# PSUM banks shared anew in a two-layer diffusion step: two banks for the prompt and the score tiles, two for the latents' single-bank products

## The chip, the cores and the metric

The kernel runs on one core of one Trainium2 chip. The metric is the device time of one execution in microseconds (us). Engines are named as in the profile: PE (TensorE matmul), PEld (its weight loads), DVE (VectorE), ACT (ScalarE), POOL (GpSimd) and SP (SyncE, which here only issues DMAs).

## The reference, cut to what matters

Two token streams go through the same two layers: 128 prompt tokens and 512 latent tokens, 1024 wide. Each layer has four mixers side by side (latent attention, a Fourier transform, gated linear attention, windowed attention), a gated merge, and a PEER block that scores every token against 16384 experts and mixes the top 16 of each of 8 heads.

```python
u = layer_norm(x) * (1 + sc1) + sh1
parts = split(u @ w_in)                  # q, k, v, gates of the four mixers
o_a, o_b, o_c, o_d = mla(parts), fourier(parts), gla(parts), swa(parts)
mix = sum(sigmoid(gate_n) * (o_n @ w_branch[n]) for n in range(4)) @ w_out
x = layer_norm(alpha * x + g1 * mix)
u = layer_norm(x) * (1 + sc2) + sh2
sc = einsum(u @ w_peer_q, peer_keys)     # two score tables of 128 keys per head
idx, w = top16(v1 + v2)
x = layer_norm(alpha * x + g2 * (w * gelu(u @ peer_u[idx])) @ peer_v[idx])
```

## The kernel before, in words

The latents come first in the program, and the prompt is a generator that is stepped beside them: each large product of the latents calls `hook()`, which adds to a credit, and for each whole credit one piece of the prompt's work is written into the program. A scheduler then orders every instruction of an engine by priority. The prompt's dense pieces of layer 0 have a priority raised by 1000, its gathers one lowered by 300; in layer 1 both are lowered. An engine runs its instructions strictly in the order that results, so an instruction that waits holds everything behind it on that engine.

PSUM has eight banks of 128x512 f32. Four of them are two double-bank buffers (`P2`: attention scores, transposes, the dense expert weights, most of the PEER output). The other four are shared between two pools. `P1` gives single-bank buffers to the latents: the 24-matmul products against streamed weights (`gemm_T`, L361), the gate product and the branch product of each merge step (L698 and L703), the root-mean-square sums (L616), the decay inputs of the gated linear attention (L793), the output projection (L1021), the scores of the PEER keys (L1115), the modulation vectors ("ada", L437), and two of the six PEER output tiles (`pout`, L1360). `PP` gives single-bank buffers to the prompt. A buffer is given out again when its last reader, on ACT or DVE, is done.

The stages of a layer for the latents: modulation and layer norm (`ln_mod`), the mixers, `attn_out`, again `ln_mod`, the choice of experts (`peer_top`: 16 products, each followed by four small score matmuls and by a selection on DVE), `wdense` (a dense matrix of expert weights, through DRAM), and the stream over 128 blocks of experts (`s_stage`, `v_stage`, `v_mm`), in which `psS` holds the scores of one block and is kept for the whole stream. In the stream the latents use `psS` and the six output tiles and nothing else.

The lines that hand out the buffers, and the one that chooses where `psS` lies:

```python
    psg = pool("psg", 4 - NPP, space=PSUM)
    psp = pool("psp", NPP, space=PSUM)
        sps = PP("psS") if NPP > 1 else P1("psS")
```

Of the kernel before, what the change touches and what calls it, by code (L numbers as in the profile page):

```python
# [49 lines left out]
SCB = 6  # L50
LND = 2
NLN = (0, 0)
NPP = 1
WPAD = 128
FILL = (2, 6)
AQ = (1, 0)
# [187 lines left out]
def build(tc, A, O, layers=L, tap=None, stop=None):  # L244
# [4 lines left out]
    def pool(name, bufs, st=top, **k):  # L249
        return st.enter_context(tc.tile_pool(name=name, bufs=bufs, **k))  # L250
# [25 lines left out]
    pss = pool("pss", 2, space=PSUM)  # L276
    psg = pool("psg", 4 - NPP, space=PSUM)
    psp = pool("psp", NPP, space=PSUM)

# [3 lines left out]
    def P1(name="p1"):  # L283
        return psg.tile([128, 512], F32, name=name, tag="g")

    def PP(name="pp"):
        return psp.tile([128, 512], F32, name=name, tag="p")
# [1001 lines left out]
    def early(l, i):  # L1289
        return NGEL - 2 + i * ((128 - NGEL + 2) // max(NEA[l], 1))  # L1290
# [34 lines left out]
    def peer(l, u, pre, raw, acc):  # L1325
# [11 lines left out]
        at = {early(l, i): i for i in range(NEA[l])}  # L1337
        sps = PP("psS") if NPP > 1 else P1("psS")
        with tc.tile_pool(name=f"wb{l}", bufs=1) as wb:
# [659 lines left out]
```

## Time and profile before

| | us |
|---|---|
| three runs, median (lowest to highest) | 4385.21 (4367.93 to 4387.62) |
| the profiled execution: its own time | 4379.12 |
| its span | 4377.0 |
| PE busy | 4177.1 |
| DVE busy | 3496.4 |
| ACT busy | 1805.2 |
| POOL busy | 1386.3 |

The profile is one execution. Its span is what the trace covers; 2.1 us lie around it. The trace shows an f32 matmul as two records, so a group of 8 records of L1556 is four matmuls. A row of the timeline ends, in brackets, with the engine's idle time before it and what ended it.

### The profile page before, as it was taken

To read this page: it belongs to the slowest core of one execution; us is meant where nothing else is said; L and a number is where in the kernel's file an instruction comes from. 1 tells how busy PE (TensorE), PEld (TensorE's weight loads), DVE (VectorE), ACT (ScalarE), POOL (GpSimd) and SP (SyncE) were. 2 spreads that over 40 slices of the span, in tenths; PEclk is the share of its full clock that TensorE was granted. 3 is DMA by queue.
4 is the path that set the end of the run, shared out by engine and by line. 5 is a ranking of instruction groups with operands and counts; after the bars stand their busy time and mean duration, and the time that the engine had idled before them with its cause. 6 is when DMAs were issued, how large, how long until landed. Compare 5 with 4: busy or idle time off the path is not lost.

```text
span 4377.0 us, 60083 instructions
## 1 busy us (share of the span) xinstructions
PE 4177.1 (95%) x21118; PEld 3324.1 (76%) x21118; DVE 3496.4 (80%) x7100; ACT 1805.2 (41%) x3109; POOL 1386.3 (32%) x1033
## 2 busy tenths in 40 slices
PE   8999999899799999999999999998889999999998
PEld 4557777674599999888886667776568889889897
DVE  3347878799898888777777687788999988878887
ACT  3344343447543333433335443434485433333333
POOL 0000433100254445244440044230004654445541
PEclk9999999999899999999999999999989999999999
DMA  7663756546899999899996576474269999999996
GB/s 247 214 211 117 260 194 212 191 131 241 302 366 338 345 343 342 278 359 337 353 351 212 174 253 224 165 233 160 82 246 345 372 369 319 335 331 348 359 333 210
DMA packets 440126, 1182.17 MB, mean 270 GB/s; under 512 B 42656, under 2 KB 152944, under 8 KB 436496
## 3 DMA queue, kind: packets, MB, share of 16 engines
q1 hardware_dynamic: 279168, 625.44, 41.1%
q0 software_dynamic: 147744, 538.10, 34.7%
q10 hardware_dynamic: 12912, 14.79, 1.0%
q8 instruction: 166, 2.72, 0.2%
q14 instruction: 136, 1.11, 0.1%
HBM read 1115.98 MB, written 62.19 MB: 269 GB/s over the span
## 4 chain that ended last, share of the span: by engine, by line
PE 67%; DVE 10%; DMA 5%; issue 3%; ACT 3%; POOL 1%; ACTq 0%; SPq 0%; DVEq 0%; POOLq 0%
PE psS L1303 23%; PE pout L1322 23%; PE p L361 8%; PE psada L444 2%; PE psw L1202 2%; DMA wraw<-in_peer_v_dram 2%; PE p L708 1%; DVE wlo L256 1%; DVE eq L256 1%; PE pp L1476 1%; PE pp L1556 1%; DMA row<-in_peer_u_dram,pidx 1%; PE p L538 1%; PE pss L673 1%; DVE y L265 1%
## 5 line engine op out<-in xcount | busy, mean ns | idle before, releaser
L350 ACT CAST whi<-wraw 128x1024 fp32r<-128x1024 f32 x694 | 728.1, 1050 | 1055.9 <-PE psS L1303 615.6
L256 DVE TENSOR_TENSOR wlo<-wraw,whi 128x1024 fp32r<-128x1024 f32 x694 | 846.6, 1220 | 385.1 <-ACT whi L350 334.4
L1303 PE MATMUL psS<-u,whi 128*128 128x384 f32 x4032 | 1051.3, 341 | 23.5 <-ACT gel L253 21.5
L1303 PEld LDWEIGHTS psS<-u,whi 128*128 128x128 f32 x4032 | 739.7, 190 | 52.2 <-ACT gel L253 27.7
L1303 PE MATMUL psS<-u,wlo 128*128 128x384 f32 x2016 | 686.3, 340 | 2.3 <-DVE wlo L256 2.3
L1218 POOL DMA_INDIRECT row<-in_peer_u_dram,pidx x256 | 325.7, 1272 | 1124.5 <-ACT pidx L1097 651.2
L361 PE MATMUL p<-u,whi 128*128 128x512 f32 (+1 forms) x1760 | 593.9, 412 | 0.7 <-DVE rt L256 0.4
L1218 POOL DMA_INDIRECT row<-in_peer_u_dram,idg x256 | 370.6, 1448 | 597.1 <-DVE dots L1229 361.0
L1218 POOL DMA_INDIRECT row<-in_peer_v_dram,pidx x256 | 323.7, 1264 | 679.0 <-DVE pacc L1235 180.0
L1218 POOL DMA_INDIRECT row<-in_peer_v_dram,idg x256 | 363.1, 1419 | 521.5 <-DVE accs L1235 443.2
L1322 PE MATMUL pout<-whi,ph 128*128 128x512 f32 x1536 | 507.5, 407 | 1.0 <-ACT whi L350 1.0
L1322 PE MATMUL pout<-wlo,ph 128*128 128x512 f32 x1536 | 501.5, 404 | 0.1
L1322 PE MATMUL pout<-whi,pl 128*128 128x512 f32 x1536 | 490.0, 398 | 0.0
L361 PEld LDWEIGHTS p<-u,whi 128*128 128x128 f32 (+1 forms) x1760 | 327.4, 190 | 88.4 <-issue 15.7
L1303 PEld LDWEIGHTS psS<-u,wlo 128*128 128x128 f32 x2016 | 381.9, 189 | 3.4 <-DVE wlo L256 2.9
L1314 ACT CAST ph<-gel 128x384 fp32r<-128x384 f32 x256 | 131.5, 514 | 574.1 <-PE pout L1322 551.9
L361 PE MATMUL p<-u,wlo 128*128 128x512 f32 (+1 forms) x880 | 360.3, 409 | 7.9 <-DVE wlo L256 7.9
L1235 DVE SCALAR_TENSOR_TENSOR pacc<-row,pdots,pacc 128x1024 f32<-128x1024 f32 x254 | 324.9, 1279 | 37.5 <-PE p L361 27.2
L1229 DVE CUSTOM_DVE_ANT_0 row<-row,pu 128x1024 f32<-128x1024 f32 x256 | 309.9, 1218 | 48.9 <-DMA row<-in_peer_u_dram,pidx 27.4
L1322 PEld LDWEIGHTS pout<-wlo,ph 128*128 128x128 f32 x1536 | 288.0, 188 | 77.2 <-issue 12.3
L1322 PEld LDWEIGHTS pout<-whi,pl 128*128 128x128 f32 x1536 | 287.7, 188 | 71.5 <-issue 4.4
L1322 PEld LDWEIGHTS pout<-whi,ph 128*128 128x128 f32 x1536 | 285.8, 188 | 59.5 <-issue 10.9
(511 smaller groups left out, 6377.2 us busy)
## 6 DMA issues: line engine op xcount, KB each, us to landing
wraw<-in_peer_ut_dram SPq DMA_DIRECT2D x256, 512.0 KB
wraw<-in_peer_v_dram SPq DMA_DIRECT2D x256, 512.0 KB
wraw<-in_w_ada_dram SPq DMA_DIRECT2D x96, 512.0 KB
wraw<-in_w_in_dram SPq DMA_DIRECT2D x96, 512.0 KB
big<-wst SPq DMA_DIRECT2D x64, 768.0 KB
pw<-in_w_gt_dram SPq DMA_DIRECT2D x128, 256.0 KB
wst<-stg SPq DMA_DIRECT2D x12, 2048.0 KB
wst<-big SPq DMA_DIRECT2D x12, 2048.0 KB
```

The costliest lines, as they stand in the source:

```text
L256: V.tensor_tensor(out=out, in0=a, in1=b, op=op)
L265: V.scalar_tensor_tensor(out=out, in0=a, scalar=s, in1=b, op0=op0, op1=op1, **k)
L350: S.copy(hi, raw)
L361: i = PE.matmul(ps[:m, :T], a[:, o:o + m], b[:, k], start=(n == 0), stop=(n == 3 * KD - 1))
L444: PE.matmul(ps[:r, :256], (s4 if split else cth)[:, 4 * hf + k, :], w[:, k * 256:(k + 1) * 256], start=(n == 0), stop=(not isg and hf == 1 ...
L1202: PE.matmul(ps[:, t * 128:(t + 1) * 128], at(oa, t), at(w, t), start=(n == 0), stop=(n == 1))
L1218: pace(G.indirect_dma_start(out=t, out_offset=None, in_=A[src], in_offset=bass.IndirectOffsetOnAxis(ap=ix, axis=0)), lags[0])
L1229: return V.tensor_tensor_reduce(out=t, in0=t, in1=x, scale=1.0, scalar=0.0, op0=ALU.mult, op1=ALU.add, accum_out=dst)
L1235: return V.scalar_tensor_tensor(out=acc, in0=t, scalar=ge, in1=acc, op0=ALU.mult, op1=ALU.add)
L1303: PE.matmul(ps, a[:, k * 128:(k + 1) * 128], b[:, k, 128:T], start=(n == 0), stop=(n == 3 * KD - 1))
L1314: S.copy(ph, ge)
L1322: PE.matmul(outs[d][hf], a[:, d * 128:(d + 1) * 128], b[:, hf * 512:(hf + 1) * 512], start=(j == 0 and i == 0), stop=(j == 127 and i == le ...
```

## The change

One constant changes. `PP`, which held one bank, holds two; `P1`, which held three, holds two; and by the line quoted above `psS` is taken from `PP` instead of from `P1`.

```diff
 NLN = (0, 0)
-NPP = 1
+NPP = 2
 WPAD = 128
```

No instruction is added or removed; the scheduler orders them anew. Three places show how.

On PE, in the prompt's first layer, where its latent attention is merged: `pp_754` and `pp_790` are the gate products of the two halves (eight matmuls each), `pp_781` and `pp_817` the branch products; `p1_1612` is a latent product and `p2_1468` the latents' Fourier transform. Before:

```order
L1556 MATMUL pp_754<-pw_776,pu_424 128x512
L361 MATMUL p1_1612<-u1_842,whi_1615 128x512
L361 MATMUL p1_1612<-u0_841,wlo_1617 128x512
L361 MATMUL p1_1612<-u0_841,whi_1615 128x512
L361 MATMUL p1_1612<-u1_842,whi_1615 128x512
L1564 MATMUL pp_781<-pw_782,pbr_752 128x512
L1564 MATMUL pp_781<-pw_785,pbr_752 128x512
L361 MATMUL p1_1612<-u0_841,wlo_1617 128x512
L361 MATMUL p1_1612<-u0_841,whi_1615 128x512
L361 MATMUL p1_1612<-u1_842,whi_1615 128x512
L361 MATMUL p1_1612<-u0_841,wlo_1617 128x512
L1556 MATMUL pp_790<-pw_791,pu_424 128x512
```

The same place in the changed kernel:

```order
L1556 MATMUL pp_754<-pw_776,pu_424 128x512
L1605 MATMUL pp_747<-p_745,pvt_723 64x128 x2
L969 MATMUL p2_1468<-dl_1477,fc_1448 128x512
L1564 MATMUL pp_781<-pw_782,pbr_752 128x512
L1556 MATMUL pp_790<-pw_791,pu_424 128x512
L1556 MATMUL pp_790<-pw_794,pu_424 128x512
L1564 MATMUL pp_781<-pw_785,pbr_752 128x512
L969 MATMUL p2_1468<-dl_1477,fc_1448 128x512
L1556 MATMUL pp_790<-pw_797,pu_424 128x512
```

The prompt's products follow one another with one or two latent matmuls between, where four stood; the latent products that stood there come later, and both orders are alike again from the last latent attention block of layer 0 on, apart from short stretches (windowed attention and gated linear attention of layer 0, the first products of its `attn_out`, the modulation products within `peer_top` and `wdense`, and the mixers of layer 1). In the two streams they are the same.

On PE, in the gated linear attention of layer 0: `p1_5082` and `p1_5088` are the two decay inputs, `p1_5325` the gate product of the next merge step, and the semaphores that an instruction waits for stand behind it. A piece of the difference:

```order
 L794 MATMUL p1_5082<-spc_1819,wg2_1440 128x512 [waits Activation_49]
 L794 MATMUL p1_5088<-spc_1819,wg2_1440 128x512 [waits Activation_49]
-L361 MATMUL p1_5325<-u0_841,whi_5328 128x512 [waits Activation_49]
+L361 MATMUL p1_5325<-u0_841,whi_5328 128x512 [waits DVE_49]
 L361 MATMUL p1_5325<-u1_842,whi_5328 128x512
-L361 MATMUL p1_5325<-u0_841,wlo_5330 128x512 [waits DVE_49]
+L361 MATMUL p1_5325<-u0_841,wlo_5330 128x512
```

Nothing moved; the wait for DVE stands two matmuls earlier, at the start of the gate product.

On PE, in `peer_top` of layer 1: `p1_26634` and `p1_26657` are two of the 16 products, `p1_26647` and `p1_26690` the score matmuls behind them. A piece of the difference:

```order
-L361 MATMUL p1_26657<-u0_25573,whi_26660 128x512 [waits PE_49,Activation_49]
+L361 MATMUL p1_26657<-u0_25573,whi_26660 128x512 [waits Activation_49]
 L361 MATMUL p1_26657<-u1_25574,whi_26660 128x512
 L361 MATMUL p1_26657<-u0_25573,wlo_26662 128x512 [waits DVE_49]
```

The order is the same; the buffer of `p1_26657` is another one, the one that `p1_26634` had two tiles earlier, where before it was that of three tiles earlier.

## Rows read from the trace of the kernel before

**Rows 1.** The page's head: span, and busy time of each engine.

```profile
span 4377.0 us, 60083 instructions
PE 4177.1 (95%) x21118; PEld 3324.1 (76%) x21118; DVE 3496.4 (80%) x7100; ACT 1805.2 (41%) x3109; POOL 1386.3 (32%) x1033
```

**Rows 2.** Busy time by stretch; columns as in its first line.

```profile
core 0: us, PE busy (x) PEld busy (x) DVE busy (x) ACT busy (x) POOL busy (x), PEclk, DMA share, GB/s
66.00:530.00 464.00, 442.74 (x2168) 293.81 (x2166) 254.31 (x672) 180.85 (x362) 48.03 (x40) 0.99 0.63 204
870.00:1026.00 156.00, 151.34 (x729) 100.31 (x729) 149.38 (x800) 67.23 (x148) 3.40 (x3) 1.00 0.46 145
1200.00:2345.00 1145.00, 1142.68 (x5674) 1000.07 (x5675) 929.16 (x1229) 420.19 (x610) 513.74 (x378) 1.00 0.94 335
3005.00:3155.00 150.00, 126.97 (x513) 86.67 (x511) 137.76 (x714) 65.22 (x129) 3.82 (x3) 0.92 0.22 71
3320.00:4377.00 1057.00, 1031.72 (x5106) 923.65 (x5105) 898.84 (x1214) 373.83 (x514) 516.31 (x370) 0.99 0.93 334
```

**Rows 3.** PE's waits over the span: for whom, us in total, times, longest.

```profile
PE p L1117 <- ACT qc L1140: 10.6, 5, 6.4
...
PE p L361 <- DVE wlo L256: 7.9, 2, 4.0
...
PE p L620 <- ACT sq L253: 4.7, 2, 4.1
...
PE p L399 <- DVE u L256: 4.2, 2, 2.3
...
PE pp L1556 <- DVE gate L265: 3.3, 1, 3.3
...
PE p L399 <- ACT u L487: 2.9, 2, 1.5
...
PE pp L1564 <- ACT gate L253: 1.7, 2, 1.0
...
PE pp L1848 <- DVE gate L265: 0.8, 1, 0.8
PE pp L1848 <- ACT pu L1849: 0.7, 1, 0.7
```

**Rows 4.** Timeline of PE: four gate matmuls of the prompt's merge.

```profile
89.65 3.70 PE L1556 MATMUL pp<-pw,pu 128*128 128x512 f32 x8
```

**Rows 5.** The chain that ended last, in time: three latent products back to back.

```profile
717.21 16.86 PE p L361 x72
```

**Rows 6.** Timeline in layer 0's gated linear attention: PE, then DVE.

```profile
631.42 0.72 PE L361 MATMUL p<-u,whi 128*128 128x512 f32 x2
636.06 0.79 PE L361 MATMUL p<-u,wlo 128*128 128x512 f32 x1 [3.92 <-DVE wlo L256]
...
634.78 2.35 DVE L256 TENSOR_TENSOR wlo<-wraw,whi 128x1024 fp32r<-128x1024 f32 x2
637.05 1.40 DVE L262 TENSOR_SCALAR zm<-p,vec 128x512 f32<-128x512 f32 x2
```

**Rows 7.** The same place in layer 1: PE, then DVE.

```profile
2804.40 0.79 PE L361 MATMUL p<-u,wlo 128*128 128x512 f32 x1 [3.96 <-DVE wlo L256]
...
2806.54 0.74 DVE L262 TENSOR_SCALAR zm<-p,vec 128x512 f32<-128x512 f32 x1
```

**Rows 8.** Timeline late in layer 1's `peer_top`: PE, then ACT.

```profile
3125.98 0.71 PE L361 MATMUL p<-u,whi 128*128 128x512 f32 x2
...
3132.62 1.16 PE L1117 MATMUL p<-ky,qc 128*128 128x128 f32 x8 [0.77 <-ACT qc L1140]
...
3131.99 0.58 ACT L1140 COPY qc<-p 128x512 f32<-128x512 f32 x1
...
3136.02 0.58 ACT L1140 COPY qc<-p 128x512 f32<-128x512 f32 x1
...
3140.03 0.23 ACT L1097 CAST idx<-fi 128x48 int32<-128x48 int16 x1 [3.05 <-DVE fi L256]
```

## The prediction

> **What bounds the kernel now.** I read the page's head first: PE is busy 4177.1 us of a span of 4377.0 [rows 1], so only about 200 us of PE's idle time can be won or lost at all, and no change of buffers makes a matmul shorter. Then I took busy time by stretch [rows 2], to see where these 200 us are. The two streams (1200 to 2345, 3320 to 4377), half of the span, leave PE idle for 1145.00 − 1142.68 = 2.3 us and 1057.00 − 1031.72 = 25 us. The mixers of layer 0, where the prompt's dense work runs beside the latents' (66 to 530), leave 464.00 − 442.74 = 21.3 us, the choice of experts in layer 0 (870 to 1026) 4.7 us, and that of layer 1 (3005 to 3155) 23 us; in the last two DVE is nearly as busy as PE or busier (149.4 of 156, 137.8 of 150), so that DVE has 6.6 and 12.2 us to spare. Third, the list of PE's waits [rows 3] tells for whom PE stood: the entry is the line that waited, then the producer or reader that ended the wait. A wait that a second prompt bank can remove is one of a `pp` product for a reader of an earlier `pp` product. Fourth, the timeline around three places where the order shows a new wait [rows 6 to 8].
>
> **The change part by part.** Nothing is added, so all costs are waits and places. All sums go against the profiled execution's own time, 4379.1 us, which is 6.1 us below the median of 4385.2.
>
> *The streams: nothing.* `psS` takes the prompt's second bank for the whole of a stream, so the prompt has one bank there as before, and the latents use no other single-bank buffer but the two `pout` tiles. PE's order is the same. What could uncover a cost is only a stream that starts in another state; it lasts 1145 and 1057 us [rows 2], and 0.1% of that is 2 us, which I keep for the range.
>
> *Gain (a): the prompt's last merge, at the end of layer 0's stream.* The prompt's gate product there waits 3.3 us for DVE's reading of the one before, and a branch product waits 1.0 us for ACT's (the L1556 and L1564 entries of [rows 3]). With two banks the gate product waits for a reader that is done earlier. I take −4.3; bounds 0 (something else is late at once, since the chunk's weights come next) and −5.7 (all of the two L1556 and L1564 entries and the L1848 one for ACT: 3.3 + 1.7 + 0.7).
>
> *Gain (b): small prompt evictions in the early part.* What remains of `pp` waits for readers is 0.7 + 0.8 for L1848 and a few tenths elsewhere; I take −1 (0 to −1.5). All `pp` waits for readers together are thus about 8 us: one bank has been nearly enough for the prompt, because between two prompt products the order puts a latent one, and such a product lasts 16.86/3 = 5.62 us [rows 5], longer than a reader takes (the comparable 128x512 copy 0.58 us [rows 8], the DVE pass 0.74 us [rows 7]).
>
> A rule speaks to this: the Trainium skill, "Perfetto Trace Analysis", section "Optimizing Tensor Performance", wants independent groups of matmuls to rotate through different banks, so that one group's eviction lies beside the next group's matmuls. By it the prompt, which had nothing to rotate through, gains; the rows agree in direction and limit it to those 8 us, and the latents still rotate, through two.
>
> *Gain (c): the prompt's dense work of layer 0 moves forward.* As the first order shows, its products lie closer together, by the end of the merges some tens of us of PE's work earlier; the latents' products fall back by as much, and by the last latent attention block the orders meet again. The sum of PE's work up to there is the same, so what is won is idle time alone: of the 21.3 us [rows 2] I count the 4.1 us that PE waits at L620 for ACT's squares [rows 3], where the prompt's gated linear attention and the latents' norms meet on ACT and now lie apart. I take −3 (0 to −4.1; the whole 21.3 is a rival below).
>
> *Loss (d): gated linear attention.* The two decay inputs now fill both latent banks, so the next gate product, whose first two matmuls ran ahead, waits for DVE to read the first (second piece of order). In layer 0 this read is the first of the two `zm` passes that begin at 637.05 and take 0.70 each, so the gate product starts at 637.75; before, it went on at 636.06, with two matmuls of 16.86/72 = 0.234 us already done [rows 5, 6]: 637.75 − 636.06 + 0.47 = 2.2 us. In layer 1 the read ends at 2806.54 + 0.74 = 2807.28 against 2804.40: 2.88 + 0.47 = 3.4 us [rows 7]. The waits for `wlo` that covered a part, 3.92 and 3.96 us, end before that, so nothing hides the rest. I take +5.6 (0, if DVE catches up the delay elsewhere, to 6).
>
> *Loss (e): `peer_top` of layer 1.* The product `p1_26657` started at 3125.98 in a third bank, while the copies of the two before it were to come. Now it needs the bank of two tiles earlier, whose copy (`qc`) starts at 3131.99 and ends at 3132.57, and on PE it is tied with the score matmuls of 3132.62; it starts at about 3133.5 and ends 5.6 us later, at 3139.1. Its own copy, which ACT took at 3136.02, is then 3.1 us late [rows 8]. Behind it on ACT stand a copy of scores and a cast that comes only at 3140.03, since it waits for DVE. The selection on DVE sets the pace there, with 12.2 us to spare, so most of it is hidden. PE already waits 10.6 us in five places for the same copy (L1117 in [rows 3]). Bounds: 0, and five heads of 3.1 us, 16 us. I take +2, nearer to 0 because DVE is 92% busy there.
>
> *Loss (f): `peer_top` of layer 0.* Here PE is nearly full (4.7 us idle). Each of the 14 products past the second may wait for a copy, at most 0.58 us where the copy comes right behind [rows 8]: 0 to 8, and I take +3.
>
> *Loss (g): the output projection.* It had three products in flight, the third starting before its input was complete; a third product's three matmuls ran ahead, 3 × 0.234 = 0.7 us [rows 5], in each layer, and PE waits at L399 for `u` for 4.2 + 2.9 us already [rows 3]. 0 to +3, and I take +2.
>
> *Loss (h): weights in bursts.* Prompt products that follow each other ask for weights faster. Four of its gate matmuls use 1 MB and took 3.70 us [rows 4], which is 285 GB/s, and with a latent product's half MB in each 5.62 us (93 GB/s) that is some 378, against 335 that the stream moves and 204 that this stretch does on average [rows 2]. Over a merge of about 17 us the lack is 17 × (378/335 − 1) = 2.2 us, unless the buffers ahead cover it. Four merges: 0 to 10; I take +2, since the mean leaves room.
>
> Sum: −4.3 − 1 − 3 + 5.6 + 2 + 3 + 2 + 2 = +6.3, so 4385.4 for an execution like the profiled one; from the median it would be 4391.5. I forecast 4388, between the two.
>
> **The rivals.** *The lost third bank decides `peer_top`* (other side, slower). If DVE's 12.2 us to spare [rows 2] are used up by the copies that come late, each further late head lengthens the stage: 16 for (e) and 8 for (f), with 5.6 for (d) and 3 for (g) some 33 us, less what (a) gives: 4379.1 + 33 − 4 = 4408, from the median 4414. For it: PE already waits at these copies. Against it: each product is 5.62 us long and the copy 0.58, and one head has two products and some 17 us of DVE's work (137.8/8), so the delay must reach DVE's input first. The Trainium skill, "Perfetto Trace Analysis", section "Identifying Performance Opportunities", says that a bubble which repeats can mean too little PSUM for the next tile; the rows show five such waits before the change, and no run yet shows more.
>
> *The early idle time goes* (faster). If the 21.3 us of the first mixers were due to the prompt being held up, an earlier prompt wins them, and with (a) 5.7: 4379.1 − 27 = 4352. Against it: of these 21.3 the waits of `pp` for readers are only a few us; the rest is for inputs.
>
> *Bursts of weights starve both* (slower, within the bound). (h) at 10 and a second such loss in the products behind: 4385.4 + 10 to 15, 4395 to 4400.
>
> *The change does nothing.* In half of the span the banks are used as before, and elsewhere a product outlasts an eviction some eightfold: 4379 to 4385.
>
> **How the numbers follow.** About 0.5%, 22 us, is what a measurement of this kernel can tell from no change; the three runs shown lie 20 us apart. From the median the bounds are 4363 and 4407. My forecast (4378 to 4397, its terms' bounds added in part) has 0.45, no effect 0.14, the bursts 0.12; together 0.71 for the same. The lost bank deciding has 0.17, and it lies past the upper bound; the early idle time 0.12, below the lower. For a range that leaves no more than 2 in 10 out I take in half of either outer case: 4364 (a large part of the early idle time won) to 4411 (the lost bank at its middle).
>
> **What would show it right or wrong.** The wait of 3.3 us of L1556 for DVE's gate is gone. In the gated linear attention a wait of L361 for DVE's `zm` (L262) stands, with about 2 and 3 us, in place of that for `wlo`. In `peer_top` new waits of L361 for ACT's `qc` (L1140) stand, and the stage of layer 1 is at most 3 us longer. The squares' wait of 4.1 us (L620) shrinks. The two streams keep 1145 and 1057 us to within 3 us. In 66 to 530, PE's idle time is 16 to 24 us, with more waits for `pw` by DMA if (h) is real. I would be wrong if the layer-0 mixers lost or won over 15 us of idle time, or if DVE's idle time in layer 1's `peer_top` grew beyond 20 us: then the buffers, not the selection, set the pace there.

## The result, and the profile after

The changed kernel took 4452.15 us (median of three, 4448.34 to 4453.02) where the kernel before took 4385.21: a ratio of 1.0156, with a 95% interval of 1.0139 to 1.0174. That is 67 us slower, past the upper end of the range, and it falls on the side of the first rival, though in other places than that rival named.

The head of the profile after, which answers to [rows 1]:

```profile
span 4446.3 us, 60082 instructions
PE 4197.9 (94%) x21118; PEld 3325.9 (75%) x21118; DVE 3500.3 (79%) x7100; ACT 1795.4 (40%) x3101; POOL 1379.6 (31%) x1033
```

PE executes as many instructions as before. (Of the kernel's own instructions none is added or removed, as said above; but in its new order ACT loads its function tables 74 times instead of 82, 94.9 us instead of 105.2.) Of the 69.3 us by which the span grew, 20.8 are PE's busy time and 48.5 its idle time. Busy time can grow without new work if the same matmuls run at a lower clock.

To see where, I cut both traces at the same products, so that each stretch holds the same stage. After (us from and to, length, then busy time of each engine, the granted clock as PEclk, and DMA):

```profile
66.00:548.40 482.40, 450.10 (x2141) 294.57 (x2140) 253.68 (x672) 176.21 (x358) 48.80 (x40) 0.98 0.60 194
548.40:905.00 356.60, 324.01 (x1500) 244.79 (x1501) 269.14 (x444) 137.59 (x239) 98.74 (x76) 0.95 0.56 191
905.00:1061.00 156.00, 150.33 (x714) 98.82 (x713) 148.81 (x799) 67.47 (x147) 3.40 (x3) 1.00 0.44 143
1061.00:1237.20 176.20, 149.76 (x1155) 93.08 (x1154) 167.39 (x457) 129.27 (x284) 23.25 (x19) 0.92 0.80 293
1237.20:2382.00 1144.80, 1139.38 (x5651) 996.26 (x5650) 920.13 (x1183) 412.21 (x599) 510.57 (x376) 1.00 0.94 335
2382.00:2437.00 55.00, 47.07 (x188) 28.47 (x187) 42.92 (x96) 30.76 (x43) 0.00 (x0) 1.00 0.73 242
2437.00:3064.00 627.00, 587.02 (x2805) 429.65 (x2804) 468.53 (x985) 230.83 (x436) 175.78 (x139) 0.98 0.62 206
3064.00:3219.00 155.00, 131.40 (x520) 88.38 (x519) 139.09 (x723) 65.99 (x130) 3.81 (x3) 0.93 0.22 71
3219.00:3382.70 163.70, 139.07 (x1104) 99.49 (x1103) 159.94 (x468) 136.06 (x305) 0.00 (x0) 0.90 0.67 241
3382.70:4446.30 1063.60, 1033.15 (x5102) 924.83 (x5100) 897.64 (x1199) 373.78 (x513) 512.15 (x370) 0.99 0.92 331
```

The stretches of before that [rows 2] does not have:

```profile
530.00:870.00 340.00, 315.77 (x1487) 242.15 (x1486) 266.23 (x443) 136.24 (x237) 97.67 (x76) 0.96 0.60 201
1026.00:1200.00 174.00, 145.45 (x1130) 87.94 (x1129) 157.98 (x410) 126.59 (x280) 22.65 (x17) 0.92 0.79 292
2345.00:2402.00 57.00, 48.66 (x182) 29.30 (x181) 43.72 (x96) 32.12 (x44) 0.00 (x0) 0.94 0.69 230
2402.00:3005.00 603.00, 581.92 (x2808) 431.33 (x2807) 465.71 (x985) 232.93 (x439) 177.56 (x139) 0.99 0.65 215
3155.00:3320.00 165.00, 143.03 (x1104) 101.92 (x1105) 159.64 (x463) 136.85 (x305) 0.00 (x0) 0.90 0.67 240
```

Read the lengths against each other. The mixers cost most of it: 482.4 − 464.0 = 18.4 us in the first part of layer 0, 356.6 − 340.0 = 16.6 in its rest with the output projection, 627 − 603 = 24 in layer 1. `peer_top` costs nothing in layer 0 and 5 in layer 1; `wdense` 2.2 and −1.3. Layer 0's stream is unchanged, the end of it 2 us shorter, and layer 1's stream 6.6 longer, which the last of the experiments takes up.

PE's waits after, for whom, in us in total, times, longest (compare [rows 3]):

```profile
PE p L361 <- DVE zm L262: 9.9, 2, 5.6
...
PE p L361 <- ACT gate L253: 7.7, 7, 1.4
PE p L370 <- ACT qc L1140: 7.2, 3, 3.3
PE p L767 <- DVE rt L256: 6.9, 2, 5.2
...
PE p L620 <- ACT sq L253: 3.7, 2, 2.3
```

The prompt's wait of L1556 for DVE's `gate` (3.3 us before) is gone. In its place latent products wait for readers of latent products: the decay inputs (`zm`), the gates of the merges, the copies of the scores' queries, and `rt`, which is DVE's reading of the rotary product `psr`. The list of before has no wait of a latent product for `zm` or for a gate, and none of L767 for `rt`.

The costliest single place is in layer 1's latent attention, PE after:

```profile
2564.19 1.02 PE L686 MATMUL psr<-qr,cst 128*128 128x512 f32 x2
2565.14 1.04 PE L686 MATMUL psr<-spc,cst 32*32 32x512 f32 x2
...
2571.79 1.22 PE L767 MATMUL p<-wukv,ckv_a 128*128 128x256 f32 x2 [5.19 <-DVE rt L256]
2573.47 1.22 PE L767 MATMUL p<-wukv,ckv_a 128*128 128x256 f32 x2 [0.46 <-ACT vt L768]
2575.15 1.22 PE L767 MATMUL p<-wukv,ckv_a 128*128 128x256 f32 x2 [0.46 <-ACT vt L768]
...
2580.19 1.22 PE L361 MATMUL p<-u,whi 128*128 128x512 f32 x2 [0.46 <-ACT vt L768]
```

and before:

```profile
2525.20 1.12 PE L686 MATMUL psr<-qr,cst 128*128 128x512 f32 x2 [0.51 <-ACT qr L746]
2526.25 1.04 PE L686 MATMUL psr<-spc,cst 32*32 32x512 f32 x2
...
2528.63 0.60 PE L767 MATMUL p<-wukv,ckv_a 128*128 128x256 f32 x2
2529.69 2.29 PE L767 MATMUL p<-wukv,ckv_a 128*128 128x256 f32 x8 [0.46 <-ACT vt L768]
```

Two rotary products fill both banks, and DVE reads the first only at 2571.05, 5.8 us after its end (before: 2.0), behind rows of the prompt's gather (L1229, 1.22 us each), for three of which it waits 2.26, 0.68 and 0.43 us until they land. Then the five value products go through the bank that came free, one by one; the last four and the gate product behind them each wait 0.46 us for the copy of the one before, while the second rotary product still holds the other bank: DVE reads it only at 2584.44.

```profile
2571.05 0.69 DVE L256 TENSOR_TENSOR rt<-psr,rtab 128x512 f32<-128x512 f32 x1
...
2584.44 0.68 DVE L256 TENSOR_TENSOR rt<-psr,rtab 32x512 f32<-32x512 f32 x1
```

From the first rotary product to the gate product it takes 16.0 us (2564.19 to 2580.19), where it took 6.8 (2525.20 to 2532.01). Nor is it idle time alone: a value product lasts 1.22 us instead of 0.60.

The granted clock there, after and before (columns as above):

```profile
2562.00:2583.00 21.00, 13.51 (x30) 6.34 (x30) 12.44 (x22) 3.84 (x9) 10.38 (x9) 0.69 0.85 296
```

```profile
2524.00:2533.00 9.00, 7.97 (x26) 3.68 (x25) 3.10 (x8) 3.79 (x9) 3.76 (x4) 1.00 0.95 354
```

A mean of 0.69 says that PE ran most of the stretch at the lower of its two levels (1.2 instead of 2.4 GHz): up to the end of the 5.19 us of idle time the mean is 0.90, and from there 0.50.

```profile
2562.00:2571.79 9.79, 4.60 (x13) 1.62 (x13) 5.79 (x12) 1.98 (x4) 4.13 (x5) 0.90 1.00 370
2571.79:2580.19 8.40, 6.09 (x10) 2.49 (x11) 3.89 (x7) 1.86 (x5) 5.12 (x4) 0.50 0.78 240
```

The two matmuls of an L361 row still take 1.05 us at 2581.63, when the waits are over, before they are back at 0.63. The Trainium skill, "TensorE: Matmul & The Clock Gate", section "A second HAM failure mode: psum-queue depth-cycling", tells of a kernel that cycles through PSUM banks and pauses so often between groups of matmuls that the clock swings between its two levels, which costs throughput. The trace agrees that such pauses go with the lower level, 0.69 against 1.00; here the clock fell once, behind one long wait and five short ones, and a swing to and fro is not shown.

### The profile page after: what moved, and what is told of

Same layout as the page of the kernel before. It is cut to its first block, busy times and chain, and to the rows that moved or that the text cites. A ratio compares the mean times of both kernels' runs of the same rounds, so it can differ in the third digit from the quotient of the medians.

```text
span 4446.3 us, 60082 instructions
## 1 busy us (share of the span) xinstructions
PE 4197.9 (94%) x21118; PEld 3325.9 (75%) x21118; DVE 3500.3 (79%) x7100; ACT 1795.4 (40%) x3101; POOL 1379.6 (31%) x1033
## 5 line engine op out<-in xcount | busy, mean ns | idle before, releaser
L361 PE MATMUL p<-u,whi 128*128 128x512 f32 (+1 forms) x1760 | 595.3, 414 | 23.4 <-DVE zm L262 9.9
L361 PEld LDWEIGHTS p<-u,whi 128*128 128x128 f32 (+1 forms) x1760 | 326.5, 190 | 122.5 <-ACT gate L253 20.7
L361 PE MATMUL p<-u,wlo 128*128 128x512 f32 (+1 forms) x880 | 359.0, 408 | 0.7 <-DVE wlo L256 0.7
L1229 DVE CUSTOM_DVE_ANT_0 row<-row,pu 128x1024 f32<-128x1024 f32 x256 | 310.2, 1220 | 60.0 <-PE p L361 31.8
L1235 DVE SCALAR_TENSOR_TENSOR accs<-row,ge,accs 128x1024 f32<-128x1024 f32 x254 | 325.9, 1283 | 5.8
```

The lines of the kernel that those rows point to most:

```text
L361: i = PE.matmul(ps[:m, :T], a[:, o:o + m], b[:, k], start=(n == 0), stop=(n == 3 * KD - 1))
L1229: return V.tensor_tensor_reduce(out=t, in0=t, in1=x, scale=1.0, scalar=0.0, op0=ALU.mult, op1=ALU.add, accum_out=dst)
L1235: return V.scalar_tensor_tensor(out=acc, in0=t, scalar=ge, in1=acc, op0=ALU.mult, op1=ALU.add)
```

## The experiments

The runs differ in the pool from which a PSUM tile comes, and the scheduler orders each anew, so no run has new pools with the old order. The diffs show the lines that matter; what stands behind # in them is a note. The lateness below is the end of one and the same PE product in the run's profile minus that in the first profile of before. `before_again`, which is the kernel before once more, shows what such a number is worth: it is off by up to 4.4 us. The columns are the end of layer 0's latent attention (479 us before), the last merge of layer 0 (783), layer 0's stream (1852), the prompt's last gate product (2380), the queries in layer 1's latent attention (2526), the last merges of layer 1 (2947), the start of layer 1's stream (3305), and the ratio of times with its interval. At 3305 the orders differ a little; at 3320, where they agree again, most of the numbers are 1 to 4 us lower (after 61.3, merge_t 6.8, long3 7.8).

```
                   479    783   1852   2380   2526   2947   3305  ratio
after             18.3   30.4   37.2   34.3   38.9   58.9   62.7  1.0156 [1.0139, 1.0174]
two_one           17.9   28.6   32.8   33.4   32.3   55.5   59.7  1.0143 [1.0125, 1.0161]
by_stage          25.5   22.5   22.7   22.9   25.0   24.1   20.7  1.0074 [1.0057, 1.0091]
decay_pk_p2       17.0   25.3   29.4   25.1   33.5   54.1   51.9  1.0139 [1.0118, 1.0159]
shared4           68.2   69.9   72.2   67.1   98.7   98.7   96.5  1.0218 [1.0201, 1.0235]
short3             8.0   19.6   21.0   22.4   23.1   38.0   37.9  1.0136 [1.0119, 1.0153]
long3              4.0    5.2    7.9    7.1    7.5    9.9   12.1  1.0040 [1.0025, 1.0055]
ada_t              7.5   19.6   24.5   24.7   26.5   51.1   54.7  1.0163 [1.0146, 1.0180]
before_short_p2    4.0    4.6    0.8    0.7    3.2    5.4    5.1  1.0027 [1.0015, 1.0039]
merge_t            0.3   -0.3   -3.6   -2.5   -3.8    5.1    8.2  1.0043 [1.0028, 1.0059]
merge_t_p2         5.5    5.6    6.4    8.7   10.4   13.1   12.7  1.0026 [1.0014, 1.0038]
lat4               6.4    2.0   -2.1   -0.7    0.9   -3.2   -3.8  0.9998 [0.9981, 1.0014]
tail4              7.0    2.9    2.0    2.7   17.2   14.0   12.7  1.0045 [1.0028, 1.0062]
before_again      -2.8   -1.8   -3.3   -1.0    0.1   -4.4   -4.3  1.0005 [0.9988, 1.0022]
```

**Whose banks: two_one.** Against the changed kernel:

```diff
-    psg = pool("psg", 4 - NPP, space=PSUM)      # NPP = 2
+    psg = pool("psg", 2, space=PSUM)            # NPP = 1
+    pst = pool("pst", 1, space=PSUM)
-        sps = PP("psS") if NPP > 1 else P1("psS")
+        sps = pst.tile([128, 512], F32, name="psS", tag="t")
```

> Two single-bank buffers for the latents as in the changed kernel, but only one for the prompt as before; psS has a bank to itself, which otherwise lies unused. Theory A (the latents lack the third bank everywhere, and the prompt's second bank gives next to nothing): as slow as the changed kernel or a few us slower, about 4452 to 4458 us: 18 us late by the end of layer 0's latent attention, some 32 late before layer 0's second layer norm, and from 2510 us on in layer 1's mixers another 22 to 28. Theory B (the prompt, running ahead with two banks, costs the 18 us of the first 480 us by bursts of weights and a lower clock): those 18 us are gone, the later losses stay, about 4435 us. Theory C (the loss is all due to the new order of the prompt's work): 4385 us.

It measured 4444.6 us, and was late by 17.9 us at 479 as the changed kernel was, although the prompt has one bank and does not run ahead. Theories B and C fall: the loss is that of the latents' third bank (waits for it, or the order that the scheduler makes without it), and the prompt's second bank is worth nothing that shows in the whole. PE's waits up to 660 us in two_one, from the same view as above, show what the two banks do in the early part:

```profile
PE p L620 <- ACT m2s L456: 5.5, 1, 5.5
...
PE p L361 <- DVE zm L262: 4.1, 1, 4.1
...
PE p L361 <- ACT gate L253: 3.2, 3, 1.8
...
PE p L767 <- ACT vt L768: 2.5, 4, 1.1
PE p L361 <- ACT vt L768: 2.5, 1, 2.5
```

The sums of the norms (L620) wait for ACT's reading of a modulation tile (`m2s`). And again half of the loss is the clock. In two_one, and then in before, over the stretch in which the early loss arises (two_one is late by 0.2 us at 228 us of before and by 20.5 at 328, two points at which both orders agree):

```profile
220.00:350.00 130.00, 110.51 (x393) 59.37 (x394) 59.21 (x96) 48.29 (x86) 0.00 (x0) 0.87 0.57 182
```

```profile
220.00:330.00 110.00, 100.92 (x398) 56.13 (x397) 52.17 (x83) 47.15 (x84) 0.00 (x0) 0.97 0.63 207
```

Of 20 us between them, 10.4 are idle time (19.5 against 9.1) and 9.6 are busy time, with about as many instructions, at a clock of 0.87 against 0.97.

**Where: by_stage.** Three pools of two, one and one bank. The last goes to the prompt up to the end of each latent attention and after layer 0's stream, and to the latents from there to the stream:

```diff
+        br_a, spc = mla(mb); third[2] = 2      # the latents' turn: every third tile
+        third[2] = 0; sps = pst.tile([128, 512], F32, name="psS", tag="t")
+            xh, outs, lnv, g2 = peer(l, u, pre, raw, acc); third[2] = 1      # the prompt's: every second
```

> The fourth single bank goes to the prompt up to the end of each layer's latent attention and after layer 0's stream, and to the latents as their third one from the end of latent attention to the stream. Theory A: late by about 18 us at the end of layer 0's latent attention as in the changed kernel, no further loss up to the stream of layer 0 (14 us fewer than the changed kernel), 3 us won at the end of that stream, and layer 1's losses of some 25 us in the mixers after 2510 and 6 us in the choice of experts gone: about 4400 us. If the later losses were due to what the prompt did before, not to the latents' banks: about 4440 to 4452 us.

It took 4413.79 us, 14 more than theory A had it, and was late by 25.5 us at 479, 7 more than expected, which no run explains. From there on it is late by 20 to 25 through both layers: where the latents have three banks, nothing more is lost. The later losses are thus not after-effects of the early part. The 3 us at the end of layer 0's stream were not won (22.7 to 22.9): the second bank seems to come after the prompt's last merge has its tiles, for L1556 still waits 3.3 us there.

**The two places that the prediction had named: decay_pk_p2.** The decay inputs and the score tiles leave the two banks:

```diff
-                ps = P1()                      # L793
+                ps = P2()[:, :512]
-                pk = P1()                      # L1115
+                pk = P2("pk")[:, :512]
```

> The changed kernel, with the two decay inputs of the gated linear attention and the score tiles of the choice of experts taken from the double-bank buffers. Theory A with its cost in the two places that the prediction named: the 9.9 us of waits for DVE's zm and some 6 us in layer 1's choice of experts go, about 4436 us. Rival (the two banks are short everywhere, a few tenths at each of the merges' products): only 0 to 6 us are won, 4446 to 4452 us.

It measured 4438.81 us, between the two. At layer 1's stream it is 62.7 − 51.9 = 10.8 us less late. Between 2947 and 3305, where layer 1's `peer_top` lies, it gains 54.1 − 51.9 = 2.2 us where the changed kernel loses 3.8. Inside `peer_top` the difference is larger: the changed kernel's lateness rises from 57.8 us (3027) to 70.6 (3113) and falls back to 62.4 by 3150, where before itself waited 6.4 us for a copy behind DVE's selection and the changed kernel 1.5; decay_pk_p2's stays at 53.4 up to 3137. Most of the loss is elsewhere.

**Could the banks be shared freely: shared4.** One pool of four, from which latents and prompt both draw:

```diff
-    psg = pool("psg", 4 - NPP, space=PSUM)
-    psp = pool("psp", NPP, space=PSUM)
+    psg = pool("psg", 4, space=PSUM)
-        return psp.tile([128, 512], F32, name=name, tag="p")
+        return psg.tile([128, 512], F32, name=name, tag="g")
```

> One pool of four single banks for prompt and latents together, so that either may hold three. Theory A (number of banks that a product finds free): the latents find a third bank whenever the prompt holds one, so the later losses go and the end of layer 0's stream gains 3 us: 4375 to 4395 us. Rival (a bank that comes in turn belongs to the slower of the two, so each waits for the other's reader): over 4410 us, with waits of the latents' L361 for readers of prompt products.

It is the slowest of all, 4477.92 us, on the side of the rival in its time: late by 68 us at 479, and another 32 are lost between 2380 and 2526. Both are stretches in which the prompt's dense work runs. Elsewhere it loses little, or gains (98.7 to 96.5). But the waits that the rival named, of the latents' L361 for readers of prompt products, are not in its list. What is there is a wait for an input:

```profile
PE pp L1490 <- ACT py L253: 20.7, 2, 13.1
```

L1490 are transposes at the prompt's layer norms; here PE comes to them before ACT has made `py`, for 7.5 us in the first stretch and 13.1 in the second, where before lost 0.3 in all. That comes of the order; what makes the rest is open.

**Which products need the third bank: short3 and long3.** Both start from two_one. In short3 the products of L738, L766, L793, L956 and L1115 (one to four matmuls) may use `psS`'s bank in turn, in long3 all others, and that includes the rotary products, of one matmul each:

```diff
+    def P3(name="p1"): cnt[0] += 1; return pst.tile([128, 512], F32, name=name, tag="t") if cnt[0] % 3 == 0 else P1(name)
-                ps = P1()                      # short3: L738, L766, L793, L956, L1115
+                ps = P3()
```

> As two_one (one bank for the prompt, two for the latents, psS's bank apart), but the latents' short products of one to four matmuls (the values and queries of latent attention, the Fourier inputs, the decay inputs, the score tiles) may use the third bank in turn; the 24-matmul products and the modulation vectors keep two. Theory D (the third bank counts where a product is shorter than its eviction): of two_one's loss of 64 us the parts in layer 1's latent attention (about 12), the gated linear attention (8), and the choice of experts (6) go, and some of the early 18: 4410 to 4422 us. Rival E (the 24-matmul products need the third bank to run ahead while ACT is late with a gate or DVE with a subtraction): no more than the decay inputs and score tiles gain, 4432 to 4445 us.

> The reverse of short3: the 24-matmul products, the branch products, the norms' sums and the modulation vectors take the third bank in turn, the short products only the two. Theory D: two_one's losses at the short products stay, 4420 to 4445 us. Rival E: nearly as fast as before, 4380 to 4400 us, with the merges and the output projection no later than before.

Short3 took 4434.86 us, long3 4394.68; both lie in the ranges of the rival E. My theory D, that short products lose because their eviction is longer than they are, explains a part at most: short3's profile is late by 37.9 us at 3305 where two_one's is by 59.7, but it is the fastest of its four executions, and the ratios are no different (1.0136, 1.0143). With the third bank for the long products 12.1 us are left. The rival E is nearer, though what it said of running ahead had still to be shown.

**One suspect: ada_t.** The modulation tiles, whose reading had held up L620, move into `psS`'s bank, except while `psS` holds it:

```diff
-        ps = P1("psada")
+        ps = pst.tile([128, 512], F32, name="psada", tag="t") if free[0] else P1("psada")
```

> As two_one, but the modulation vectors lie in psS's bank except while psS holds it, so they take none of the latents' two. Theory F (the early 18 us, up to the end of layer 0's latent attention, come because a modulation tile holds one of two banks over its eviction on ACT, its two small matmuls and its read on DVE, and the latents' products have one left): late by less than 6 us there, and about 4430 us in all. Rival (the early loss is that of the merges' gate and branch products with each other): still 14 to 18 us late there, 4440 us and more.

Late by 7.5 us at 479, between the two expectations: about 10 of the early 18 us are these tiles'. In the rest it loses what two_one loses or more, and as a whole it is no faster, 4447.76 us.

**The other suspect: merge_t.** Only the gate products of the merges get `psS`'s bank, all to themselves:

```diff
-                    ps = P1()                  # L698, the gate product of a merge step
+                    ps = pst.tile([128, 512], F32, name="pgate", tag="t")
```

> As two_one, but the gate products of the latents' merges alone lie in psS's bank (before and after psS); all other latent products keep two. Theory G (a merge's gate product is written in pieces as filler between the steps of the attentions, holds a bank for 9 to 45 us where it takes 5.6 back to back, and so leaves the rest one bank): most of two_one's loss of 64 us in the mixers goes, with the losses in the choice of experts (7) left: 4395 to 4415 us. Rival (no one kind of product is the cause, all need three in turn): the gate products, with only one bank of their own, wait for ACT's reading at each step, and 4425 us or more remain.

That is nearly enough: no loss at all up to 2526 us, 8.2 left at 3305, 4399.12 us, in the range of theory G. Since the tile now has a name of its own, one sees how it is written. Busy time of the instructions of `pgate` alone:

```profile
340.00:380.00 40.00, 8.97 (x28) 4.99 (x26) 0.60 (x1) 0.98 0.43 133
380.00:420.00 40.00, 4.05 (x10) 1.67 (x10) 0.60 (x1) 1.00 0.43 134
2666.00:2674.00 8.00, 6.37 (x24) 4.30 (x24) 0.00 (x0) 1.00 0.88 268
```

In 80 us of layer 0 PE spends 13 on gate products; one of them is written from 349.1 to 396.0 us, a few matmuls at a time between the steps of the attention. Of the 64 gate products 44 last longer than 7 us from the first matmul to the last, and the median is 9.0, where 24 matmuls back to back take 5.62 [rows 5]; I worked this out from the first and last matmul of each. The products that bear one name in the other kernels, counted off by 24, show the same: in the changed kernel 46 of the 110 last longer than 7 us, the longest 60.8. A bank is taken from the first matmul on, so for much of the mixers one bank belongs to a product under way, and with two the short products around it have one.

At the costliest place it is the other way round: there the rotary products hold both banks, and no gate product can be written while PE waits. In merge_t the value products also go through one bank, one after the other, but matmuls of a gate product stand between them:

```profile
2525.72 0.59 PE L767 MATMUL p<-wukv,ckv_a 128*128 128x256 f32 x2
2525.97 0.82 PE L361 MATMUL pgate<-u,whi 128*128 128x512 f32 x2
2526.63 0.39 PE L361 MATMUL pgate<-u,wlo 128*128 128x512 f32 x1
2526.86 0.62 PE L767 MATMUL p<-wukv,ckv_a 128*128 128x256 f32 x2
```

From 2510 to 2538, two points at which the orders agree, the changed kernel loses 12.0 us, two_one 11.8, short3 8.8, long3 4.6, merge_t none. That DVE is late does not decide it: its first reading comes 5.8 us after the product's end in the changed kernel, 6.7 in short3 and 6.9 in long3 (2.4 in merge_t), and in long3 a gate product is written meanwhile. What each of the two ways costs over the whole kernel, no run tells apart.

**Is that all: merge_t_p2.** merge_t with the edits of decay_pk_p2:

> merge_t (the merges' gate products in psS's bank, two banks for the other latent products, one for the prompt), and the decay inputs and the score tiles from the double-bank buffers. If theory G's gate products, the decay inputs and the score tiles are together all that the third bank was needed for, the late 8 us of merge_t at layer 1's stream go, 4376 to 4388 us, no different from before. If something else in layer 1 needs it too, 6 us and more stay, 4390 us and more.

Layer 1's `peer_top` and `wdense` no longer lose (13.1 to 12.7, where merge_t went from 5.1 to 8.2; inside `peer_top` the lateness stays at 14.4 from 3027 to 3137, where merge_t's rises from 6.4 to 19.2). But it took 4392.75 us, on the side of the second expectation: the whole is still 0.26% slower than before, 11 us, and its profile was late by 5.5 at 479. What makes these is open.

**A faster version: before_short_p2, lat4, tail4.** before_short_p2 is the kernel before with the short products of L738, L793, L956 and L1115 taken from the double banks:

> The kernel before with its one prompt bank and three latent banks, where the queries of latent attention, the Fourier inputs, the decay inputs and the score tiles are taken from the double-bank buffers, which makes a fourth and fifth place. Theory A: PE's waits for the copies of the scores' queries (10.6 us before) shrink and the whole is 4 to 10 us faster than before, about 4375 us. Rival (three banks were enough, and what sets the pace of the choice of experts is DVE's selection): 4380 to 4386 us, no change.

4388.19 us, 0.27% slower, and the waits for the copies of the scores' queries do not shrink (11.2 us, before 10.6). Whether what goes to the double banks collides there is not shown. lat4 is the kernel before with a fourth bank for the latents after each latent attention; tail4 also gives the prompt a second bank after layer 0's stream:

```diff
+        four[0] += 1; return PP(name) if four[1] and four[0] % 4 == 0 else psg.tile([128, 512], F32, name=name, tag="g")
+                hook(); third[2] = 2           # tail4: here the prompt's second bank goes back
```

> The kernel before, but from the end of each layer's latent attention to the stream the latents also take the prompt's bank in every fourth turn. If a fourth bank helps as the third did: some us in the merges and 3 to 8 us in layer 1's choice of experts, 4368 to 4378 us. If three are enough: 4378 to 4388 us, the same as before.

> lat4, and the prompt takes psS's bank from the end of layer 0's stream to the end of that layer. Gain (a) of the prediction by itself: 2 to 4 us less than lat4 by the first products of layer 1, so 4366 to 4384 us in all; if the prompt's new order costs the latents as much, the same as lat4.

lat4 is no different from before, so three banks are enough from the end of latent attention on. tail4 is 0.45% slower: its lateness rises from 2.7 to 17.2 us between 2380 and 2526, and one wait makes that:

```profile
2427.99 1.97 PE L1490 MATMUL pp<-cst,py 128*128 128x128 f32 x8 [14.24 <-ACT py L253]
```

As in shared4, PE comes to the prompt's transposes before ACT has made their input. Nor does tail4 test gain (a): the prompt's second bank seems to come after the tiles of its last merge, for L1556 still waits 3.4 us for DVE's gate, as before. No version was found that beats the kernel before.

**What the profiles of one kernel differ by: before_again.**

> The kernel before, unchanged, for a second profile of it. Layer 1's stream took 6 to 9 us longer in the profiles of most variants than in that of before, whichever banks they had. If that is scatter between executions, this profile too differs from the first by several us there, or reaches the end of the stream's first 300 us late; if it belongs to the variants, it is the same to within 2 us.

Layer 1's stream, cut at the same products as in [rows 2]:

```profile
3316.00:4380.00 1064.00, 1033.49 (x5106) 925.59 (x5104) 898.73 (x1212) 373.71 (x513) 511.19 (x370) 0.99 0.92 331
```

It took 1064 us in the second profile of the same kernel and 1057 in the first. The 6.6 us of the changed kernel there need thus not be the change's.

## Why the prediction was wrong, step by step

**The step that failed** is what the sum leaves out. The latents' products in the mixers, the decay inputs apart, stand in it at nothing, on the ground that stands under its rivals, that "elsewhere a product outlasts an eviction some eightfold", 5.62 us against 0.58. That holds for a product written back to back and read at once. In the mixers the scheduler writes the gate products in pieces, with a median of 9.0 us and up to 46.9 (merge_t), and a rotary product waits 5.8 us for DVE, which is behind the prompt's gather. The changed kernel is late by 18.3 us at 479, by another 10 at 783 and by another 19 from 2510 to 2947, the decay inputs not counted: some 48 of the 67 us, of which 12.0 come at the one place with the rotary and value products. I had looked at the waits of before, where three banks hide this, and in the order only at places where a wait is new in name. And my list of those who use the latents' banks, in the kernel before in words, lacks among others the rotary products (L686), the queries (L740), the values (L767) and the Fourier inputs (L958), which come from `P1` too.

**What a wait costs** was the second gap: I priced each in idle time, and held that only PE's idle time can be won or lost. In the early part of two_one the lower clock costs 9.6 us beside 10.4 of idle time; over the whole of the changed kernel PE's busy time grew by 20.8.

**Gain (a)**, −4.3: the waits are gone, and from 2347 to 2378 us the changed kernel gains 36.8 − 34.6 = 2.2 us and decay_pk_p2, the other run without them, 29.3 − 26.0 = 3.3, while two_one, which waits 3.5 us there, loses 0.9. Right in its mechanism, too large in its size. The prompt's waits for readers that the prediction adds up to "about 8 us" are 3.3 + 1.7 + 0.8 + 0.7 = 6.5 in [rows 3]; one of 0.7 is counted in both gains.

**Gains (b) and (c)**: too small to be told apart; the wait at L620 went from 4.1 us to 2.3, but the idle time of the stretch grew by 11.0.

**Loss (d)**, +5.6: the waits for `zm` are there, 4.35 and 5.6 us in place of those for `wlo`. From 627 to 641 us the changed kernel's lateness rises from 20.3 to 22.1, and from 2799 to 2812 from 52.3 to 54.2, 3.7 us in all; in decay_pk_p2, where these inputs lie elsewhere, it falls from 19.0 to 17.6 and from 47.2 to 45.3. The mechanism was right and the size about right.

**Losses (e) and (f)**, +2 and +3: layer 1's `peer_top` is 5.0 us longer and layer 0's no longer. Their sum came out by luck, since (f) cost nothing and (e) more than its +2. The mechanism of (e) was right: PE falls behind by 12.8 us within the stage, and at its end, where before waited for the selection, all but about 4 are won back; with the score tiles elsewhere the loss goes. The waits stand at L370 (7.2 us) rather than at L361. **Loss (g)**, +2: in layer 0 the output projection adds 32.0 − 30.4 = 1.6 us (its last product, by the same comparison), within the scatter, and in layer 1 nothing. **Loss (h)**, +2: the waits for the prompt's weights (`pw`) between 66 and 660 us did grow, from 4.8 to 8.6 us, but in two_one, with one prompt bank, they are 10.9; so they are not those of a prompt that runs ahead. Whether they make a part of the 18 us in either kernel is not shown.

**The signs.** The wait of L1556 is gone and those for `zm` and `qc` stand, as forecast. Layer 0's mixers lost 11.0 us of idle time in the first part and 8.4 in the rest up to the choice of experts, 19.4, past the 15 by which the prediction said that it would be wrong.

**The rivals.** The lost third bank did decide, with the cost of the first rival (4414) and another 38 us, but not in `peer_top`, and its condition, that DVE's time to spare be used up, is not what happened (DVE's idle time in layer 1's is 15.9 us after, 12.2 before). The prompt ahead did not win the early idle time; that stretch's grew from 21.3 to 32.3.

## What to carry to other kernels

In this program a PSUM bank is taken from the first matmul of a group to the end of its last reader. Where a scheduler spreads a group as filler between other work, count that span, not the group's length back to back, before taking a bank away; a name of its own for such a tile makes the span visible. List every user of a pool that shrinks, stage by stage, short products above all, and look for readers that stand in a long queue. Ask also what the engine can do while such a reader is awaited: in long3 and merge_t a product with a bank of its own filled the time that the changed kernel lost.

## What the runs showed that was not expected

In two places a stall cost about as much again in slower matmuls: 0.69 instead of 1.00 in the granted clock over 21 us around one 5.19 us wait and five of 0.46, with the value products at 1.22 instead of 0.60 us; and 9.6 us of busy time beside 10.4 of idle time in two_one. Over the whole kernel it was less, 20.8 us beside 48.5. And a pool that gives the prompt more banks can hurt by the order alone: in tail4 and shared4 PE stands at the prompt's transposes for 14.2 and 13.1 us, for an input that ACT has not made, where the kernel before waits 0.3 us in all.
